# Three places in the order of a two-layer encoder's mixer: the spread of the norm's row, the state products, the second rotary queries

## The chip, the cores and the metric

The kernel runs on one core of a Trainium2 chip. The metric is the time of one execution on the device in microseconds (us); lower is better. A run of the kernel gives one time, and the median of several is compared.

## The reference, cut to what matters

Two layers act on 576 columns of tokens: 512 of a new prompt and 64 of a running stream. A layer is a feed-forward stage, a mixer and a second feed-forward stage, each with a norm in front and behind:

```
x = x + 0.5 * post1(SwiGLU_1(pre1(x)))
h = pre2(x); z = h @ w_in[l]
mix = concat[MLA(512) | HGRN2(256) | chunk-gMLP(256)] @ w_out[l]
x = x + post2(mix)
x = x + 0.5 * post3(SwiGLU_2(pre3(x)))
```

The change lies in the mixer. MLA is attention with four heads, in which queries have a plain and a rotary part, and keys and values come from a compressed latent, for the running stream also from a cache of 256 rows. HGRN2 is a gated recurrence with a matrix state, S_new = exp(b_last) * S + (k * exp(b_last - b))^T v in chunks. A norm needs, for each token, 1/sqrt(mean of squares), which is then multiplied into everything computed from the token.

## The kernel before, in words

**Layout.** x stands as eight tiles of 128 features by 576 tokens; the tokens are two halves of 288 columns (`HALF`). Each fp32 matrix is split into a rounded high part and a rest, so that one product is three matrix multiplications (`three`). PSUM has one pool of eight banks, tag `mm`, from which every product, transpose and column sum takes its bank (`mm`, `sm`); a bank comes free when the engine that copies it out has done so. SBUF is one pool of 57 equal slots.

**How the order is made.** The order is written by hand as a planner in the code. The main line emits the big products; smaller chains are Python generators that are put into a list with a due time (`spawn`). The planner has a clock `self.t`, to which each emitted product adds an estimate: its columns divided by 2400 (in us), at least 0.107. After each group of products `tick` emits every generator step that is due, and a step says with `yield v` that its next one is due v later on that clock. Where the main line needs a result, `until` emits the step with the earliest due time, again and again, while the clock stands still apart from what the steps themselves add:

```
    def until(self, done):
        while not done():
            self.step(min(self.bg, key=lambda q: q[0]))
```

The framework then builds one queue for each engine. Emission order is its priority; where it reckons an instruction not to be ready, a later one may go ahead. At run time each engine takes its queue in that order.

**The norm in front of the mixer.** `post` finishes a half of the stage before and emits its eight parts of h (1.3 of the clock apart for the second half); then `pre_stats` waits 3.97 (first half) or 7.0 (second half), takes column sums of squares with TensorE, scales them on VectorE (`m`, L209), takes the power -0.5 on GpSimd (`rn`, L151), and after `yield 3.11` spreads the row over 128 partitions with three transposes (`spread`, tile `bc`) and copies it to `rbc` with ScalarE (L215). The mixer's first products, four `u` banks for each half, run over eight groups of 12 multiplications (1.44 of the planner's clock each). `zout(z, o, half)` needs `rbc` and empties the four banks; its first line is

```
        self.until(lambda: hf in self.stats_done)
```

For the first half `zout` stands right behind the last group of that half; for the second half it stands behind `natural(nch, 0, 512)`, whose eight groups of three products of 512 columns count 0.64 each. After that `hgrn` starts.

**The state part.** In `hgrn`, behind the levels, `ed[m]` (two tiles) is transposed in five pieces each (tile `tp`), copied by ScalarE to `kdn[m]` (L799) and `kd` (L803), one m after the other with `yield 1.5`. Then ten state products `su` follow 1.2 apart, in the order m = 0, m = 1 for each of five token tiles, each with two VectorE updates, the first and last also with DMAs of the state to HBM, eight in a layer. Behind them come five `out(i)`, 3.2 apart: products `o`, a group norm (ScalarE square, VectorE sum, GpSimd power, VectorE `on`, L847), and 9.0 later transposes into `mixh` and `mixl`. `gates` polls until `ed` is there, and then has ScalarE do five gelu and five silu in a row.

**The values and rotary queries.** `value(j)` is six products of 512 columns into one bank and one VectorE copy (L1171); j = 0 to 4 are new tokens, 5 and 6 the cache. `rope(u)` is a query product of two banks with nine multiplications each (`query`), eight ScalarE copies of 32 rows (`sw`, L1146), two VectorE products with cosT, one GpSimd product with sinT (L1148), a VectorE sum (L1149), and a split with four ScalarE copies and two VectorE differences (`low`, L1156). The order is value 0, 1, rope(4), value 2 to 4, rope(5), value 5, 6. Then for each head `query(h)` (two banks, `q`) with its split (`qh`, `ql`), and keys `k` (three banks).

Of the kernel before, what the change touches and what calls it, by code (L numbers as in the profile page):

```python
# [41 lines left out]
def tcol(i):  # L42
    return 0 if i == 0 else 64 + P * (i - 1)


def twid(i):
    return 64 if i == 0 else P


class Net:  # L50
# [149 lines left out]
    def pre_stats(self, half, wait, sums=None):  # L200
        nc = self.nc
        c0, n = HALF[half]
        nt = 3
        t0 = 3 * half
        rn, rn2, rbc, acc = self.rn, self.rn2, self.rbc, self.acc
        yield wait
        ps = self.colsum(acc, RUNS[half]) if sums is None else sums[:, 2 * half:2 * half + nt]
        m = self.small("m", 6)
        nc.vector.tensor_scalar(m[:, :nt], ps[:, :nt], 1.0 / D, EPS, op0=ALU.mult, op1=ALU.add)  # L209
        r = rn[:, t0:t0 + nt]  # L210
        self.rsqrt(r, m[:, :nt], nt)
        nc.vector.tensor_tensor(rn2[:, t0:t0 + nt], r, r, op=ALU.mult)
        yield 3.11
        bc = self.spread(r, half, None if sums is None else tuple((tcol(i), twid(i)) for i in range(2 * half, 2 * half + nt)))
        nc.scalar.activation(rbc[:, c0:c0 + n], bc, AF.Copy)  # L215
        self.stats_done.add(half)
        if sums is not None and half == 0:

            yield 1.0
            ps = self.sm("ru")  # L220
            self.mul(ps[:, 0:1], rbc[0:1, W2 - P:W2], self.ones[0:1, 0:1], start=True, stop=True)
            nc.vector.tensor_copy(rn[:, 2:3], ps[:, 0:1])
            nc.vector.tensor_tensor(rn2[:, 2:3], rn[:, 2:3], rn[:, 2:3], op=ALU.mult)
# [432 lines left out]
    def hgrn(self, l, zq, zf, vg):  # L656
# [137 lines left out]
        for m in range(2):  # L794
            kdn[m] = self.slot("kdn")[:, :512]
            ps = self.sm("tp")
            for i in range(1, 5):
                self.flip(ps[:, (i - 1) * P:i * P], ed[m][:, tcol(i):tcol(i) + P])
            nc.scalar.activation(kdn[m], ps, AF.Copy)  # L799
            kdn[m, 0] = self.small("kd0", P, 2)  # L800
            ps = self.sm("tp")
            self.flip(ps[:64, :P], ed[m][:, :64])
            nc.scalar.activation(kdn[m, 0][:64], ps[:64, :P], AF.Copy)  # L803
            yield 1.5
        while len(vg) < 5:
            yield 2.07
        for i in (1, 2, 3, 4, 0):
# [244 lines left out]
    def mixer(self, l, gpost, gpre, nxt, packed):  # L1052
# [80 lines left out]
        def query(u):  # L1133
            ps = [self.mm("q"), self.mm("q")]
            for k in range(3):
                for (c0, n), pp in zip(HALF, ps):
                    self.three(pp[:, :n], wqh[k][:, u], wql[k][:, u], qah[k][:, c0:c0 + n], qal[k][:, c0:c0 + n], k == 0, k == 2)
                self.tick()
            return ps

        def rope(u):
            ps = query(u)
            t, sw = self.slot("q"), self.slot("sw")
            for (c0, n), pp in zip(HALF, ps):
                for g in range(4):
                    nc.scalar.activation(sw[g * 32:(g + 1) * 32, c0:c0 + n], pp[(g ^ 1) * 32:((g ^ 1) + 1) * 32, :n], AF.Copy)  # L1146
                nc.vector.tensor_tensor(t[:, c0:c0 + n], pp[:, :n], cosT[:, c0:c0 + n], op=ALU.mult)
            nc.gpsimd.tensor_tensor(sw, sw, sinT, op=ALU.mult)  # L1148
            nc.vector.tensor_tensor(t, t, sw, op=ALU.add)  # L1149

            low = self.slot("low", F32R)
            for e in range(2):
                s, o = slice(64 * e, 64 * e + 64), slice(64 - 64 * e, 128 - 64 * e)
                qr = self.slot("qr", F32R)
                nc.scalar.activation(qr[s], t[s], AF.Copy)
                nc.vector.tensor_tensor(low[s], t[s], qr[s].bitcast(F32), op=ALU.subtract)  # L1156
                nc.scalar.activation(qr[o], low[s].bitcast(F32), AF.Copy)
                a["qr"].append(qr)

        def value(j):  # L1160
            t = self.slot("v")
            ps = self.mm("v")
            for ct in range(2):
                if j < 5:
                    xh, xl = cth[ct][:, tcol(j):tcol(j) + P], ctl[ct][:, tcol(j):tcol(j) + P]
                else:
                    xh, xl = c["ch"][:, ct, (j - 5) * P:(j - 4) * P], c["cl"][:, ct, (j - 5) * P:(j - 4) * P]
                self.mul(ps, xh, uw[0][:, ct], ct == 0, False)
                self.mul(ps, xh, uw[1][:, ct], False, False)
                self.mul(ps, xl, uw[0][:, ct], False, ct == 1)  # L1170
            nc.vector.tensor_copy(t[:, :512], ps)  # L1171
            (a["v"] if j < 5 else a["vc"]).append(t)
            self.tick()
# [4 lines left out]
        rope(4)  # L1178
        for j in range(2, 5):
            value(j)  # L1180
        rope(5)
        self.finish([cg])
        for j in range(5, 7):
            value(j)
        uk = self.chunk([(slice(None), tin["mla_w_uk"][l].rearrange("(k p) h n -> p k (h n)", p=P))], 2, 512)
        at = self.spawn(self.attention(a, c))
        for h in range(HEADS):
# [284 lines left out]
```

## Time and profile before

| | us |
|---|---|
| median of 3 runs | 2253.6 |
| lowest and highest of them | 2252.36, 2254.13 |
| the profiled execution's own time | 2250.07 |
| its span, first to last instruction | 2248.3 |
| TensorE busy in it | 2194.2 |
| mean granted TensorE clock | 0.995 of full speed |

The profiled execution is one run; 1.8 us of its time lie outside its span, and it is 3.5 us below the median. The two mixers reach TensorE at about 415 and 1525 us of the span; times below are counted from the span's start. A row of the timeline gives the start, the duration, the engine, the line, and in brackets how long the engine had been idle and what ended that.

### The profile page before, as it was taken

To read this page: it belongs to the slowest core of one execution; us is meant where nothing else is said; L and a number is where in the kernel's file an instruction comes from. 1 tells how busy PE (TensorE), PEld (TensorE's weight loads), DVE (VectorE), ACT (ScalarE), POOL (GpSimd) and SP (SyncE) were. 2 spreads that over 40 slices of the span, in tenths; PEclk is the share of its full clock that TensorE was granted. 3 is DMA by queue.
4 is the path that set the end of the run, shared out by engine and by line. 5 is a ranking of instruction groups with operands and counts; after the bars stand their busy time and mean duration, and the time that the engine had idled before them with its cause. 6 is when DMAs were issued, how large, how long until landed. Compare 5 with 4: busy or idle time off the path is not lost.

```text
span 2248.3 us, 39455 instructions
## 1 busy us (share of the span) xinstructions
PE 2194.2 (98%) x15988; PEld 2140.4 (95%) x15988; DVE 1540.6 (69%) x2805; ACT 1054.0 (47%) x1877; POOL 69.5 (3%) x96
## 2 busy tenths in 40 slices
PE   8999999999999999999999999999999999999998
PEld 8999999988899999999999999998888999999998
DVE  5888743686766988845498875437867579787543
ACT  7444442344564645443265454325356546444423
POOL 0000000101200000000000000000011000000000
PEclk9999999999999999999999999999999999999999
DMA  7333442222112333344223334423121223323421
GB/s 218 96 97 94 116 143 81 84 69 79 57 57 81 101 98 98 87 130 127 66 81 104 94 93 125 135 76 108 34 85 52 74 98 89 97 86 107 119 71 43
DMA packets 339250, 210.79 MB, mean 94 GB/s; under 512 B 17350, under 2 KB 319420, under 8 KB 339068
## 3 DMA queue, kind: packets, MB, share of 16 engines
q1 hardware_dynamic: 339068, 208.28, 31.0%
q8 instruction: 125, 2.05, 0.4%
q14 instruction: 57, 0.47, 0.1%
HBM read 189.85 MB, written 18.38 MB: 93 GB/s over the span
## 4 chain that ended last, share of the span: by engine, by line
PE 87%; DVE 7%; ACT 3%; POOL 2%; issue 2%; DMA 0%; SPq 0%; POOLq 0%; DVEq 0%; ACTq 0%
PE d L68 25%; PE X L68 20%; PE Q L68 10%; PE u L68 9%; PE R L68 5%; PE n L68 5%; PE wo L68 4%; PE sc L68 1%; PE lv L68 1%; POOL gr L151 1%; PE oT L68 1%; PE q L68 1%; DVE hl L142 1%; DVE wl L127 1%; PE k L68 1%
## 5 line engine op out<-in xcount | busy, mean ns | idle before, releaser
L68 PE MATMUL d<-gh,wh 128*128 128x288 f32 x1408 | 413.5, 297 | 2.7 <-ACT gh L138 2.7
L68 PE MATMUL d<-gl,wh 128*128 128x288 f32 x1408 | 413.9, 295 | 0.0
L68 PE MATMUL d<-gh,wl 128*128 128x288 f32 x1408 | 412.7, 294 | 0.0
L127 DVE TENSOR_TENSOR wl<-wr,wh 128x1024 fp32r<-128x1024 f32 (+3 forms) x190 | 220.3, 1164 | 179.2 <-ACT wh L126 178.8
L126 ACT ACTIVATE wh<-wr 128x1024 fp32r<-128x1024 f32 (+3 forms) x190 | 191.7, 1012 | 315.7 <-PE d L68 167.3
L68 PEld LDWEIGHTS d<-gh,wh 128*128 128x128 f32 x1408 | 262.3, 187 | 3.6 <-ACT gh L138 3.6
L68 PEld LDWEIGHTS d<-gh,wl 128*128 128x128 f32 x1408 | 264.7, 188 | 0.0
L68 PEld LDWEIGHTS d<-gl,wh 128*128 128x128 f32 x1408 | 264.1, 188 | 0.0
L68 PE MATMUL X<-th,wh 128*128 128x288 f32 x864 | 255.7, 296 | 0.0
L68 PE MATMUL X<-tl,wh 128*128 128x288 f32 x864 | 254.9, 295 | 0.0
L68 PE MATMUL X<-th,wl 128*128 128x288 f32 x864 | 254.0, 294 | 0.0
L68 PE MATMUL u<-hl,wh 128*128 128x288 f32 x736 | 219.5, 299 | 4.4 <-DVE hl L142 4.4
L68 PE MATMUL u<-hh,wh 128*128 128x288 f32 x736 | 217.9, 303 | 3.4 <-ACT x L1376 2.4
L68 PE MATMUL u<-hh,wl 128*128 128x288 f32 x736 | 219.2, 299 | 0.6 <-DVE wl L127 0.6
L138 ACT ACTIVATE wh<-wr 128x1024 fp32r<-128x1024 f32 x144 | 151.4, 1055 | 134.7 <-PE R L68 68.4
L139 DVE TENSOR_TENSOR wl<-ws,wh 128x1024 fp32r<-128x1024 f32 x108 | 132.3, 1225 | 95.6 <-ACT wh L138 95.6
L398 DVE TENSOR_TENSOR d<-d,d 128x288 f32<-128x288 f32 x128 | 55.2, 454 | 181.9 <-PE d L68 181.7
L139 DVE TENSOR_TENSOR wl<-wr,wh 128x1024 fp32r<-128x1024 f32 x144 | 174.8, 1220 | 7.2 <-ACT wh L138 6.2
L138 ACT ACTIVATE wh<-ws 128x1024 fp32r<-128x1024 f32 x108 | 114.5, 1060 | 138.3 <-DVE ws L508 100.7
L68 PEld LDWEIGHTS X<-th,wl 128*128 128x128 f32 x864 | 162.7, 188 | 0.0
L68 PEld LDWEIGHTS X<-tl,wh 128*128 128x128 f32 x864 | 162.2, 188 | 0.0
L68 PEld LDWEIGHTS X<-th,wh 128*128 128x128 f32 x864 | 161.9, 187 | 0.0
(363 smaller groups left out, 5401.9 us busy)
## 6 DMA issues: line engine op xcount, KB each, us to landing
wr<-ffn_w_gate SPq DMA_DIRECT2D x144, 256.0 KB, 3.0
wr<-ffn_w_up SPq DMA_DIRECT2D x144, 256.0 KB, 3.4
wr<-ffn_w_down SPq DMA_DIRECT2D x64, 512.0 KB, 4.2
wr<-w_in SPq DMA_DIRECT2D x30, 512.0 KB, 3.7
xd<-x SPq DMA_DIRECT2D x48, 288.0 KB, 2.1
x<-xd SPq DMA_DIRECT2D x48, 288.0 KB, 6.2
wr<-ffn_w_down SPq DMA_DIRECT2D x32, 384.0 KB, 3.5
wr<-ffn_w_gate SPq DMA_DIRECT2D x16, 512.0 KB, 3.8
```

Source lines behind the costliest of these rows:

```text
L68: self.nc.tensor.matmul(out, lhsT, rhs, start=start, stop=stop, skip_group_check=onto)
L126: nc.scalar.activation(hi[:, :a * b], raw[:, :a * b], AF.Copy)
L127: nc.vector.tensor_tensor(lo[:, :a * b], raw[:, :a * b], hi[:, :a * b].bitcast(F32), op=ALU.subtract)
L138: nc.scalar.activation(hi, src, AF.Copy)
L139: nc.vector.tensor_tensor(lo, src, hi.bitcast(F32), op=ALU.subtract)
L142: nc.vector.scalar_tensor_tensor(lo, src, scale, hi.bitcast(F32), op0=ALU.mult, op1=ALU.subtract)
L151: self.nc.gpsimd.tensor_tensor(out, m, self.mhalf[:, :n], op=ALU.pow)
L398: nc.vector.tensor_tensor(d[m][:, sl], d[m][:, sl], ps[hf][:, :n], op=ALU.add)
```

## The change

Three edits, which only alter the order of emission. `self.packed` is false in `pre_stats` only where the stage that follows is the mixer.

```diff
@@ pre_stats
         nc.vector.tensor_tensor(rn2[:, t0:t0 + nt], r, r, op=ALU.mult)
-        yield 3.11
+        yield 3.11 if self.packed else 5.5
         bc = self.spread(r, half, None if sums is None else tuple((tcol(i), twid(i)) for i in range(2 * half, 2 * half + nt)))
@@ hgrn
             nc.scalar.activation(kdn[m, 0][:64], ps[:64, :P], AF.Copy)
-            yield 1.5
+            yield 3.5
         while len(vg) < 5:
@@ mixer
         rope(4)
         for j in range(2, 5):
             value(j)
-        rope(5)
         self.finish([cg])
         for j in range(5, 7):
             value(j)
+        rope(5)
```

## Rows read from the trace of the kernel before

**Rows 1.** The page: busy time of TensorE, and the chain that ended last.

```profile
PE 2194.2 (98%) x15988; PEld 2140.4 (95%) x15988; DVE 1540.6 (69%) x2805; ACT 1054.0 (47%) x1877; POOL 69.5 (3%) x96
PE 87%; DVE 7%; ACT 3%; POOL 2%; issue 2%; DMA 0%; SPq 0%; POOLq 0%; DVEq 0%; ACTq 0%
```

**Rows 2.** Busy time by stretch: length, then busy us (count) of each engine, clock, DMA.

```profile
456.00:596.00 140.00, 132.40 (x826) 116.51 (x825) 105.70 (x308) 65.58 (x137) 15.14 (x19) 1.00 0.24 69
...
740.00:1515.00 775.00, 771.65 (x5790) 770.10 (x5789) 532.00 (x766) 348.12 (x547) 6.59 (x6) 1.00 0.34 101
```

**Rows 3.** TensorE's waits over the span: total us, times, longest.

```profile
PE bc L73 <- POOL rn L151: 8.4, 2, 4.2
PE q L68 <- DVE v L1171: 5.4, 4, 2.7
...
PE su L68 <- ACT kdn L799: 3.9, 2, 2.0
...
PE su L68 <- DVE cn L908: 2.1, 1, 2.1
```

**Rows 4.** Timeline of the first layer, the first half's statistics.

```profile
429.70 0.72 PE L68 MATMUL ss<-ones,acc 128*128 128x1 f32 x6
...
433.68 0.15 DVE L209 TENSOR_SCALAR m<-ss 128x3 f32<-128x3 f32 x1
...
434.81 0.98 PE L73 MATMUL bc<-ident_c,rn 64*128 64x64 f32 x3 [4.15 <-POOL rn L151]
```

**Rows 5.** Three short stretches; the last three columns are granted clock, DMA share, GB/s.

```profile
434.80:438.50 3.70, 3.69 (x16) 3.57 (x17) 3.70 (x11) 2.12 (x5) 0.00 (x0) 0.50 0.43 160
...
546.00:550.00 4.00, 3.88 (x28) 3.88 (x29) 2.18 (x12) 2.32 (x9) 1.52 (x2) 1.00 0.01 4
...
619.50:624.00 4.50, 4.48 (x21) 4.44 (x22) 4.21 (x10) 3.33 (x10) 0.00 (x0) 0.62 0.38 111
```

**Rows 6.** Timeline of the first layer, the second half's spread and what follows it.

```profile
450.46 0.49 PE L73 MATMUL bc<-ident_c,rn 128*128 128x128 f32 x3
...
452.70 1.54 DVE L1050 TENSOR_TENSOR z<-u,rbc 128x288 f32<-128x288 f32 x4
...
457.22 1.28 ACT L672 ACT_TABLE_LOAD   x1
```

**Rows 7.** Timeline of ScalarE in the first layer, around the copies of kdn.

```profile
543.95 1.64 ACT L893 ACTIVATE vg<-vg 128x256 f32<-128x256 f32 x5
545.50 0.57 ACT L799 ACTIVATE kdn<-tp 128x512 f32<-128x512 f32 x1
```

**Rows 8.** Timeline of TensorE in the first layer, the second transposes and their product.

```profile
539.49 0.71 PE L73 MATMUL tp<-ident_c,e 128*128 128x128 f32 x5
...
546.12 0.49 PE L68 MATMUL su<-vg,kdn 128*128 128x128 f32 x2 [1.95 <-ACT kdn L799]
```

**Rows 9.** The chain that ended the stretch 600 to 640: start, us, what.

```profile
614.84 1.45 POOL sw L1148
...
618.79 0.69 DVE v L1171
619.52 2.47 PE q L68 x9
```

**Rows 10.** Timeline of ScalarE and VectorE, where head 0's query is split.

```profile
619.61 0.41 ACT L138 ACTIVATE qh<-q 128x288 fp32r<-128x288 f32 x1
...
621.01 0.82 DVE L139 TENSOR_TENSOR ql<-q,qh 128x288 fp32r<-128x288 f32 x2
```

**Rows 11.** TensorE's waits over the stretch 1530 to 1830, the second layer's mixer.

```profile
PE q L68 <- DVE v L1171: 1.6, 1, 1.6
```

**Rows 12.** Groups by line, 565 to 600 us: us and mean ns, then idle time before.

```profile
L847 DVE SCALAR_TENSOR_TENSOR on<-o,gr,vg 128x64 f32<-128x64 f32 x20 | 4.3, 277 | 3.7 <-POOL gr L151 3.7
...
L141 ACT ACTIVATE mh<-tp,colg 128x128 fp32r<-128x128 f32 (+1 forms) x7 | 2.5, 356 | 2.6 <-PE tp L73 2.3 <-DVE ml L142 0.2
L634 ACT ACTIVATE gsq<-o 128x256 f32<-128x256 f32 x5 | 1.9, 381 | 1.2 <-DVE gs L637 1.2
```

## The prediction, made before the change was run

> **What bounds the kernel now.** First the page: TensorE is busy 98% of the span and makes up 87% of the chain that ended last [rows 1]. VectorE, ScalarE and GpSimd have slack on average, so a reordering can only win back TensorE's idle time. The stretches then say where that lies: between 740 and 1515 us TensorE lacks 3.4 of 775, and a multiplication takes 775/5790 = 0.134 us there; in 456 to 596, inside the first mixer, it lacks 7.6 of 140 [rows 2]. The list of TensorE's waits names the causes. Three groups stand where the three edits act: the spread `bc` behind the power `rn` (8.4 us, two times), the second query behind the copies of the values (5.4), the state products behind `kdn` (3.9) [rows 3]. Together 17.7 us, 0.8% of the span, and no more than that plus the clock is to be had.
>
> The clock adds to it. Behind the 4.15 us wait of `bc` the granted clock is 0.50, that is 1.2 GHz, and 16 multiplications take 3.70 us instead of 16 x 0.134 = 2.1; behind the 2.7 us wait of the second query it is 0.62 on average, and 21 take 4.5 instead of 2.8; behind the 1.95 us wait of a state product it is 1.00 [rows 4, 5, 8]. So the longest waits cost another 1.6 to 1.7 each, the shorter ones nothing.
>
> **Edit 1, the spread: nothing.** It names the largest wait, so it has to be followed by hand. First half: the column sums are emitted one tick before the last group of the half's products, which adds 12 x 0.12 = 1.44 to the planner's clock. Then the main line reaches `zout` for the first half, and its `until` empties the generators with the clock standing still. Before, the spread is due 3.11 - 1.44 = 1.67 past that moment, now 5.5 - 1.44 = 4.06. Its only rival there is the second half's `post`: its remaining parts are due at 1.3, each in turn, and behind them its statistics at 7.0. 1.67 and 4.06 both lie between 1.3 and 7.0. So in both versions the rest of the parts comes first, the spread second, and no product in between: the order of emission up to there is the same, and the 4.15 us of `bc` in the first layer, of which 434.81 - 430.42 = 4.4 us runs from the end of the column sums (VectorE reaches `m` only at 433.68 behind the other half's parts), stays with its slow clock [rows 4, 5]. The second layer has the same code and the same kind of wait (8.4 in two) [rows 3].
>
> Second half: here the spread is emitted by a tick. At 3.11 it falls behind the last group of `u`, at 5.5 two steps of `natural` later (2 x 0.64 = 1.3 on the planner's clock). Nothing waits there now, the row of `bc` has no idle time in front, so there is nothing to gain [rows 6]. What may be lost is hidden: `z` needs the row, ends at 452.70 + 1.54 = 454.24, and ScalarE starts its table for `hgrn` at 457.22 behind the first `natural`; 3.0 us of cover for a shift of 1.3 [rows 6]. Without that cover it would cost 1.3 in each layer. I take 0; bounds 0 and +2.6.
>
> **Edit 2, the state products: -3.9.** The second transposes are done at 540.2, but ScalarE holds its queue with gelu and silu until 545.59 and only then copies `kdn`, to 546.07; the product of m = 1 stands waiting 1.95 us [rows 7, 8]. The edit moves the second transposes 2 later, the first product of m = 0 and m = 1 about 4 later on the planner's clock. The ten matrix multiplications and their 20 VectorE updates move along, and the eight state DMAs; behind these on the SP queue stand loads of weights and of cosT, wanted only by the rotary queries of the stretch behind 600 [rows 9], so their cost is nothing; if that lead were gone, rope(4) would wait by the same 4. The copy of `kdn` may now stand behind a square (0.38) and one norm's worth of small ScalarE work, about 1 us later; the product comes 4 us later, so 4 - 1 = 3 is more than the 1.95. The wait goes, in both layers: -3.9 [rows 3]. What is late next is the bank for a later state product, which VectorE frees with `cn` (2.1 us) [rows 3]. That chain starts from `natural` products that themselves come 1.95 earlier, so I let it stand as it is; bounds: 0 if it takes back all, -3.9 - 2.1 = -6.0 if it goes as well.
>
> **What follows from edit 2: +2.0.** The five `out(i)` and their transposes also come about 4 later, a little over one spacing of 3.2, so one out more falls among values and rotary queries. One out costs VectorE 4 x 0.277 and more, ScalarE 0.381 + 2 x 0.356 = 1.1 [rows 12]. Between 600 and 619.5 the chain runs through ScalarE's `sw` copies, GpSimd, VectorE and back and TensorE hangs on its end [rows 9], so work put into these queues can lengthen it. No row shows how much lands in gaps. I take +1.0 for each layer; bounds 0 and +2.2 (1.1 on each of the two engines, one after the other) each.
>
> **Edit 3, the cached values first: -3.6.** No instruction is added: 12 products and two copies change places with one rope (18 multiplications, 12 ScalarE, 5 VectorE, one GpSimd). VectorE works in the order given, so the copies of values 5 and 6 now stand between the parts of rope(5), which wait for ScalarE and GpSimd: `sw` ends at 616.29, value 5 is copied at 618.79, and the bank it frees lets the second half of `query(1)` start at 619.52, 2.7 late [rows 9]. With values 5 and 6 in front, both copies (0.69 each) fall into the time in which VectorE waits for rope(5), and TensorE passes 619.52 - 2.7 = 616.8 without a stop. It then does nine multiplications of `query(1)` and six of `k`, 15 x 0.134 = 2.0, to 618.8, and there lacks a bank again: all are held by `q` and `k` of head 0, which ScalarE and VectorE split behind rope(5), at 619.61 and 621.01 [rows 10]. With the two copies out of VectorE's way the first `ql` comes 0.7 to 1.4 earlier, and half of 0.82 later the bank is free, at 620.0 to 620.7. The new wait is 1.2 to 1.9; I take 1.5, which is nearer to the 1.95 behind which the clock stayed at full speed than to the 2.7 [rows 5]. Queued behind it are the rest of `k(1)` and head 0's scores. First layer: -2.7 - 1.7 + 1.5 = -2.9; bounds -4.4 and 0. Second layer: the same wait is 1.6 [rows 11]; I take off under half, -0.7, bounds -1.6 and +0.6 (rope(5)'s product is emitted two values later, and ScalarE could start late). Sum -3.6.
>
> A page bears on the 1.7. The Trainium skill, "TensorE: Matmul & The Clock Gate", section "HAM oscillation", says that an idle gap of TensorE shuts its clock to half rate for what follows, but counts only gaps longer than this one. By it the 2.7 us wait would cost itself alone and the sum be 1.7 smaller, -3.8. This trace shows 0.62 behind that wait, so the row decides.
>
> **Sum.** 0 - 3.9 + 2.0 - 3.6 = -5.5 us: 2250.07 becomes 2244.6 for an execution like the profiled one, whose span would be 2242.8. The median of the runs lies 3.5 above it: 2253.6 - 5.5 = **2248.1**. That is 0.24%; about 0.2%, 4.5 us, is what a measurement can tell from no change.
>
> **The rivals.**
> - Edit 1 bites. If the build's own ordering lets a few products of the next half pass the spread, 2.39 of planner's clock is some 20 multiplications, 2.7 us: the wait falls from 4.15 to 1.5 and the clock stays. 2.7 + 1.55 = 4.2 for each layer, 8.5 together: 2239.6. For: it is the largest wait. Against: the emission does not change. 0.10.
> - The gain is handed on. The wait for `kdn` reappears at the bank behind `cn`, or the outs take what rope gains: about -1, 2252.6. For: that wait of 2.1 us stands on the same state products [rows 3]. 0.20.
> - The clock is not won back. If TensorE's new stop at `k(1)` is as long as the old one, half speed follows as now, and 1.7 of edit 3 is lost: 2249.8. For: rows 5 leave open what a wait between 1.95 and 2.7 does. 0.12.
> - Slower. One mechanism: the shifted outs hold their banks among the values and queries until their norm is done, and TensorE meets a new wait of the size of `bc`'s, 4.15 with 1.55 of slow clock, in each layer: +11.4 - 5.5 = +5.9, 2259.5. It decides from 5.0 for each layer. For: VectorE stands idle 3.7 us before the `on` of this stretch, for GpSimd, so a bank is held long [rows 12]. 0.12.
>
> **Numbers.** The forecast has 0.46, and nine tenths of it lie beyond 4.5 us, with rival one: 0.51 faster. Rivals two and three and the rest of the forecast: 0.37 within 0.2%. Slower: 0.12. Likeliest own range 2243 to 2252. The bounds of the terms reach from -6.0 - 4.4 - 1.6 = -12 to +2.6 + 4.4 + 0.6 = +8; the 8-in-10 range takes in rival one and stops short of rival four: 2239.5 to 2256.
>
> **What would show it.** In the new profile: `bc` behind `rn` still about 8.4 in two (edit 1 does nothing); no wait of `su` for `kdn`; no wait of `q` for `v` L1171 at the second query, but one of `k` for `ql` or `qh` of 1 to 2 us, with the clock at 1.00 behind it; waits on `on` not above today's. The forecast is wrong if `bc`'s wait shrinks, or if waits of `v`, `q` or `u` for `on` grow by several us.

## The result, and the profile after

The changed kernel takes 2265.8 us (median of four runs, 2262.3 to 2266.6) against 2253.3; the ratio is 1.0053, with a 95% interval of 1.0035 to 1.0070. It is slower by 12 us, where 5.5 less were forecast. The profiled execution took 2262.28 us with a span of 2260.5, 12.2 longer than before.

The page after, its line of busy time:

```profile
PE 2203.1 (97%) x15988; PEld 2149.3 (95%) x15988; DVE 1540.2 (68%) x2805; ACT 1054.5 (47%) x1877; POOL 71.3 (3%) x96
```

The same 15988 instructions keep TensorE busy 8.9 us longer than in [rows 1]; the other engines' work is the same. So 8.9 of the 12.2 us are not waits, but instructions that run longer, and 3.3 are more idle time. Some ends of multiplications are modelled, so the split is rough; but it says where to look: at the granted clock.

TensorE's waits after, in the form of [rows 3] (total us, times, longest):

```profile
PE bc L73 <- POOL rn L151: 8.4, 2, 4.2
PE u L68 <- DVE ml L139: 4.9, 2, 2.5
PE sc L68 <- ACT kth L138: 4.4, 2, 2.2
...
PE q L68 <- DVE v L1171: 3.9, 2, 2.0
PE q L68 <- DVE on L847: 3.7, 2, 1.9
PE tp L73 <- DVE ctl L139: 2.9, 2, 1.5
```

The spread's wait stands as it was. The state products wait for `kdn` no more, nor for the bank behind `cn`; transposes wait 2.9 for `ctl` in place of 0.9. New are a unit of q_a behind `ml`, head 0's scores behind the split of its keys, and a query behind `on`; the query behind `v` is a single wait of 2 us in each layer now.

What follows such a wait is seen in stretches of 4 us, the first layer (us, busy us and multiplications, granted clock, DMA share, GB/s):

```profile
576.10:580.10 4.00, 3.97 (x20) 0.65 0.17 45
592.00:596.00 4.00, 3.91 (x26) 1.00 0.46 139
597.60:601.60 4.00, 3.96 (x19) 0.57 0.83 266
616.80:620.80 4.00, 3.94 (x19) 0.68 0.42 124
629.00:633.00 4.00, 4.00 (x30) 1.00 0.00 0
```

and the second layer:

```profile
1689.70:1693.70 4.00, 3.96 (x18) 0.57 0.07 12
1710.00:1714.00 4.00, 4.00 (x19) 0.57 0.79 268
1729.10:1733.10 4.00, 3.93 (x20) 0.74 0.42 125
1741.30:1745.30 4.00, 3.97 (x15) 0.58 0.01 4
```

But for the one from 592.0, which has no wait ahead of it, the stretches begin where a wait ends: for `ml` (576.1, 1689.7), `on` (597.6, 1710.0), `v` (616.8, 1729.1) and `kth` (629.0, 1741.3). Seven of eight run partly at 1.2 GHz, behind waits of 1.7 to 2.5 us; the eighth, from 629.0, is at 1.00 although its wait was 2.2 us.

The start of the n-th multiplication, counted from the first of each trace, after minus before (us). Where the order differs it is not the same product in both, so values inside the mixers are good to about half a us:

```
position before:  540    561    569    577    596    606    620    629 to 1533
after - before:   1.75  -0.91  -0.56   4.65   6.34   6.72   5.07   5.94 to 5.89
position before: 1652   1671   1688   1697   1709   1730   1739 to the end
after - before:   5.86   3.74   7.98   6.91   6.34   8.33  12.2
```

1.1 us were there before the first mixer. Edit 2 wins its 2 us in each layer as forecast, to be seen at 561 (2.7) and 1671 (2.1). At 577 and at 1688 they are lost twice over. The last step, 8.33 to 12.2 between 1730 and 1739, is the second layer's wait for `kth` and the half clock behind it.

### The profile page after: what moved, and what is told of

It reads as the page before. It is cut to its first block, busy times and chain, and to the rows that moved or that the text cites. A ratio compares the mean times of both kernels' runs of the same rounds, so it can differ in the third digit from the quotient of the medians.

```text
span 2260.5 us, 39439 instructions
## 1 busy us (share of the span) xinstructions
PE 2203.1 (97%) x15988; PEld 2149.3 (95%) x15988; DVE 1540.2 (68%) x2805; ACT 1054.5 (47%) x1877; POOL 71.3 (3%) x96
## 4 chain that ended last, share of the span: by engine, by line
PE 86%; DVE 7%; ACT 3%; POOL 2%; issue 2%; DMA 0%; SPq 0%; POOLq 0%; DVEq 0%; ACTq 0%
PE d L68 25%; PE X L68 20%; PE Q L68 10%; PE u L68 9%; PE R L68 5%; PE n L68 5%; PE wo L68 4%; PE sc L68 1%; PE lv L68 1%; POOL gr L151 1%; PE oT L68 1%; PE q L68 1%; DVE hl L142 1%; DVE wl L127 1%; PE k L68 1%
```

## What stands at 576 us

TensorE and VectorE of the changed kernel there (start, us; in brackets idle time and what ended it):

```profile
572.83 0.48 PE L68 MATMUL su<-vg,kd 64*128 64x128 f32 x2
573.24 0.44 PE L73 MATMUL tp<-ident_c,kp 128*128 128x128 f32 x2
576.13 0.40 PE L68 MATMUL u<-hh,wh 128*128 128x288 f32 x1 [2.45 <-DVE ml L139]
```

```profile
575.01 0.87 DVE L864 SCALAR_TENSOR_TENSOR uv<-uv,gr,cmlp_v_g 128x64 f32<-128x64 f32 x4 [0.95 <-POOL gr L151]
575.80 0.28 DVE L139 TENSOR_TENSOR ml<-tp,mh 128x128 fp32r<-128x128 f32 x1
576.11 0.29 DVE L821 SCALAR_TENSOR_TENSOR st<-st,eb,su 64x64 f32<-64x64 f32 x1
576.43 0.69 DVE L139 TENSOR_TENSOR ccl<-tp,cch 128x512 fp32r<-128x512 f32 x1
577.04 0.28 DVE L877 SCALAR_TENSOR_TENSOR oc<-cm,colg,uv 128x64 f32<-128x64 f32 x1
```

Counted from the trace, all eight banks are held at 575.0: two by the unit before, one by a gated product's transposes, two by the last state products, two by the transposes of the cached latents (`ck`) and keys (`kp`), one by `cm`. All but the unit's two wait for VectorE next, and it takes them in its queue's order: it stands behind `uv`, which waits for GpSimd's power. The transposes of the caches are due at a fixed time of the planner's clock; the state products, moved by 4, have run into them: the last product starts at 572.83, behind the transposes of `ck` from 571.43. Before, they were just through: the last product started at 566.90, its updates ended at 572.48, and the transposes of `ck` began at 572.50.

## Experiments: each edit alone

**Edit 1 alone.**

```diff
-        yield 3.11
+        yield 3.11 if self.packed else 5.5
```

> Only the first edit (the yield in front of the spread). Theory S (the state products' move made the kernel slower): no change, 0 +- 3 us, with the two waits of bc for rn still 4.2 us each, since the first half's spread is emitted at the same place. Theory V (the order of values and rope did): the same. Rival (the spread's later place delays what starts the recurrence): +3 us or more, with waits of dq and lv above the 0.4 to 0.8 of before.

Measured: 2251.3, ratio 0.9992 (0.9982 to 1.0001), no change. `bc` waits as before:

```profile
PE bc L73 <- POOL rn L151: 8.3, 2, 4.2
```

**Edit 2 alone.**

```diff
             nc.scalar.activation(kdn[m, 0][:64], ps[:64, :P], AF.Copy)
-            yield 1.5
+            yield 3.5
```

> Only the second edit (3.5 instead of 1.5 behind each transpose of ed). Theory S: +6 to +12 us: the two waits of su for kdn (1.95 each) go, and in their place come waits of u and q of 1.7 to 2.5 us behind VectorE, each with some 4 us of clock at half speed. Theory V: -2 to -4 us, the waits for kdn gone and nothing in their place.

Measured: 2266.7 (2259.6 to 2267.5), ratio 1.0048 (1.0032 to 1.0064), within the error the whole loss. The five executions are two at 2259.6 and 2260.2, at a mean granted clock of 0.991, and three at 2266.7 to 2267.5, at 0.986 to 0.987; the median stands in the upper group, so the ratio says more. The waits of one from the lower group:

```profile
PE q L68 <- DVE on L847: 5.1, 4, 2.0
PE u L68 <- DVE ml L139: 4.9, 2, 2.5
```

**Edit 3 alone.**

```diff
-        rope(5)
         self.finish([cg])
         for j in range(5, 7):
             value(j)
+        rope(5)
```

> Only the third edit (values 5 and 6 in front of rope(5)). Theory S: -1 to -4 us, the waits of q for v L1171 (2.7 and 1.6) replaced by a shorter one. Theory V: +6 to +12 us, with a new wait of sc for kth of 2.2 us in each layer and half clock behind it.

Measured: 2251.5, ratio 0.9994 (0.9985 to 1.0003), no change. The query's wait for `v` is gone from the list; in its place stands

```profile
PE sc L68 <- ACT kth L138: 5.1, 2, 3.3
```

with 3.3 us in the first layer and a stretch at 0.68 behind it:

```profile
624.00:628.00 4.00, 3.99 (x18) 0.68 0.00 0
```

ScalarE does rope(5)'s copies first and splits head 0's keys only at 623.3. The wait moved on, and its clock with it.

**Edits 2 and 3.**

> The second and third edit without the first. Both theories: as the full change, +9 to +14 us, since the first edit does nothing; if it comes out under +5, the first edit has a share.

Measured: 2265.0, ratio 1.0050 (1.0035 to 1.0065): edit 2 alone, within the error. Edit 2 is the cause; what is open is what in it.

## Experiments: banks or outs, and how much is the clock

**Edit 2, the caches' transposes 4 later as well.**

```diff
 def caches(self, l, c):
...
-        yield 14.0
+        yield 18.0
```

> Edit 2 alone, and with it the transposes of the cached latents and keys come 4 later on the planner's clock as well (18 in place of 14), so that they stand where they stood to the last state products in the kernel before. Theory B (banks): edit 2 loses because the last state products meet those transposes, and the banks of both wait for VectorE; here the wait of a unit for ml, 2.45 us in each layer, shrinks to under 1.2, the half-clock stretches behind it at 577 and 1690 go, and the time falls from 2266.7 (edit 2 alone) by 5 to 9 us to 2258 to 2262. Rival O (outs): the loss comes from the five outs that are pushed among the values and queries, whatever the caches do; then the time stays at 2264 to 2268 and a query still waits about 2 us for on.

Measured: 2257.1, ratio 1.0021 (1.0011 to 1.0030). By the ratios about half of the loss goes, with the outs due where edit 2 puts them; the unit's wait for `ml` is gone from the list, and where it was the clock is 1.00. The queries' waits for `on` fall too, from 5.1 to 1.4, the longest from 2.0 to 0.7: rival O, which had them stay at 2, fails, and most of that wait too hangs on where the caches' transposes stand. What is left shows in a later stretch: a wait of 1.35 us for the rotary keys' split `kptl`, and half clock behind it.

```profile
576.00:580.00 4.00, 4.00 (x34) 1.00 0.19 45
587.20:591.20 4.00, 3.71 (x16) 0.57 0.41 134
```

**Half of edit 2.**

```diff
-            yield 1.5
+            yield 3.5 if m else 1.5
```

> Edit 2 for its second half alone: the transposes of m = 1 stand where they stood before, the state products follow 2 later (yield 3.5 only behind m = 1), half of edit 2's shift of the products and outs. Theory B: products and outs move by 2, and what counts is whether the last ones reach the caches' transposes; the stretch behind them is between the two kernels, 2255 to 2262, with a unit's wait for ml of 0.5 to 1.5 us. Rival T (transposes): the moved transposes do the harm, since the copies of kdn then stand behind ScalarE's other work; here they are not moved and the time is the one before, 2252 to 2255. A third way: a threshold, either 2253 or 2266.

Measured: 2256.2, ratio 1.0014 (1.0004 to 1.0023), in between, as theory B had it, but by other waits than it named: 0.3 us for `ml`, 1.3 for `kpt` in the first layer and 2.4 for `kptl` in the second, among the transposes of the caches and of the rotary keys.

**Work in the wait.** Edit 2 with idle transposes ahead of the unit that waits:

```diff
             self.flip(ps[:, t * P:(t + 1) * P], kp[:, t * P:(t + 1) * P])
+        for _ in range(14):
+            self.nc.tensor.transpose(ps[:, 256:384], kp[:, :P], self.ident)
```

> Edit 2 alone, with 14 more transposes in each layer, into an unused part of the bank of the cached keys' transposes, right ahead of the unit that waits 2.45 us. They add 28 transposes, some 4 us of TensorE's work, and change no result. Theory C (clock): about 4 us of edit 2's loss is not the two waits but the half clock behind them; with TensorE at work instead of waiting the clock stays at 1.00 behind 577 and 1690 and the time falls by some 4 us below edit 2 alone, to 2261 to 2264, although work is added. Rival W (waits alone): the clock doesn't follow the wait; the time is that of edit 2 alone or up to 4 longer, 2266 to 2271.

Measured: 2257.9, ratio 1.0023 (1.0014 to 1.0033): 8.8 us less than the median of edit 2 alone, 5.6 by the ratios, on another chip, with 28 transposes more.

**The same work where nothing waits.**

```diff
                     ps = self.mm("wo")
+                    if k0 == 4 and mm == 3 and hf == 0:
+                        for _ in range(14):
+                            nc.tensor.transpose(ps[:, 320:448], self.ident, self.ident)
```

> Edit 2 alone with the same 14 transposes in each layer, but where TensorE has no wait: ahead of a product of w_out, behind the mixer. The control to the run with them in the wait. Theory C (clock): these transposes only cost their time, 28 x 0.15 = 4.2 us, and the half clock behind the waits stays: 2268 to 2272. Rival P: any 28 transposes, wherever they are, change the time as much, because the build orders other things differently with them; then about 2258, as with the ones in the wait.

Measured: 2262.0, ratio 1.0044 (1.0029 to 1.0059), which neither theory gave. So the three, edit 2 alone, the work in the wait and the work elsewhere, were run once more on one chip.

> Edit 2 alone once more, on one chip with the next two, since it was timed on another chip than the kernels with added transposes and its five runs there fell into two groups (2259.6 to 2260.2 at a granted clock of 0.991, 2266.7 to 2267.5 at 0.986 to 0.987). Theory C (clock): the groups are those executions in which the clock fell behind more or fewer waits; the median lies between 2258 and 2267, and within the runs the lower clock goes with the longer time. Rival W: the edit costs the same at any clock, 2263 to 2267 here too.

> Edit 2 alone with the 14 transposes in the wait of each layer (28 x 0.109 = 3.1 us of work, by the trace). Theory C: 3 to 7 us below edit 2 alone on this chip, and 5 to 8 below the same work elsewhere. Rival W: the work fits into the wait, nothing else changes: the time of edit 2 alone within 1 us, and 3 below the same work elsewhere.

> Edit 2 alone with the same 28 transposes behind the mixer, where TensorE doesn't wait. Both theories: 3 us above edit 2 alone on this chip. If it comes out below edit 2 alone again, as it did across two chips, then adding work anywhere moves the clock in other stages too, and the two comparisons above are no measure of the one wait.

Measured: edit 2 alone 2263.4 (2262.0 to 2266.0; ratio 1.0048, 1.0035 to 1.0061), work in the wait 2257.4 (2252.9 to 2258.1; 1.0020, 1.0011 to 1.0029), work elsewhere 2262.4 (2258.6 to 2264.6; 1.0040, 1.0027 to 1.0053). The work in the wait takes 6.0 us off, within theory C's 3 to 7. The same work elsewhere comes out 5.0 above it, where theory C had 5 to 8. The first layer's two stretches, edit 2 alone:

```profile
575.20:579.20 4.00, 3.95 (x18) 0.58 0.18 45
595.40:599.40 4.00, 3.90 (x19) 0.61 0.80 278
```

and with the work in the wait:

```profile
578.20:582.20 4.00, 3.90 (x29) 1.00 0.18 45
597.00:601.00 4.00, 3.91 (x32) 1.00 0.80 278
```

29 multiplications in place of 18 in the same 4 us, and 32 in place of 19. The first wait is down to 0.93 us, with transposes in the time that was idle:

```profile
575.68 1.69 PE L586 MATMUL tp<-ident_c,kp 128*128 128x128 f32 x14
578.30 0.40 PE L68 MATMUL u<-hh,wh 128*128 128x288 f32 x1 [0.93 <-DVE ml L139]
```

The second wait, a query's for `on`, is as long as ever (1.96 us at 597.1), and the clock stays at full speed behind it all the same. The earlier pair of traces, edit 2 alone and the work in the wait on two other chips, agrees with this pair on all four places (both layers).

The work elsewhere came out 1 us below edit 2 alone, where 3 above was expected (the two intervals overlap). By what was written ahead of it, added work then moves the clock in other places too, and the 6.0 us is no clean measure of these waits. Where it stands the work costs 1.5 us in each layer, 14 x 0.109; but the profiled execution of edit 2 alone has a half-clock stretch at 1142 us, outside the mixers, which costs it 3.1, and that of the work elsewhere has none. The last section comes back to that stretch. The profiled execution with the work in the wait has it too, so it makes no difference between those two.

What the traces do show is where the clock fell. Between 540 and 660 us and between 1650 and 1770, TensorE was at 1.2 GHz for 6.8 us in all in the kernel before, for 27.3 in the changed kernel (where waits for `v` and `kth` come on top), for 17.1 in both traces of edit 2 alone, for 13.6 in both with the work elsewhere, and not at all in both with the work in the wait. Half of 17.1 - 6.8 is 5.1 us, my estimate of what half clock adds to edit 2; it is near the 6.0.

## Experiments: the wait that edit 1 aimed at

**Units ahead of the row.** The kernel before, with products put where edit 1 wanted them:

```diff
-        for hf in (0, 1):
-            o = self.units(chs, hf)
-            if hf == 0:
-                self.zout(z, o, 0)
+        o = self.units(chs, 0)
+        o1 = self.units(chs[:2], 1)
+        self.zout(z, o, 0)
+        o = o1 + self.units(chs[2:], 1)
+        o1 = None
```

> The kernel before with the mixer's first units in another order: behind the first half's four units come the second half's products of the first two units, then the first half is scaled by its row, then the other two units. So products really stand between the column sums and the spread, which edit 1 aimed at and did not do. If the reading of edit 1 is right (the row's wait is there only because nothing may be emitted between), the two waits of bc behind rn, 8.3 us together, and the half clock behind each go, in part to small waits of a unit for VectorE's parts: the time falls by 4 to 9 us to 2244 to 2249. Rival: TensorE follows VectorE's parts of the second half there anyway, with four or with two units, and the waits only spread: within 2 us of the time before.

Measured: 2247.4 (2242.3 to 2251.6), ratio 0.9977 (0.9967 to 0.9987), 5 us faster than before, and so faster than both kernels. The column sums end at 432.3 and products of the second half fill the time to 436.3. The row, and the stretch around it:

```profile
436.69 0.63 PE L73 MATMUL bc<-ident_c,rn 64*128 64x64 f32 x3 [0.44 <-POOL rn L151]
```

```profile
436.00:440.00 4.00, 3.33 (x23) 1.00 0.40 152
```

0.44 us in place of 4.15, at full clock where [rows 5] had 0.50. Over the row's stretch the trace gains 4.2 us in the first layer and 4.35 in the second.

**The same with work in two more waits**, in each layer 12 transposes ahead of the first state product of m = 1 and 12 ahead of query(1):

```diff
+                if i == 1 and m == 1:
+                    for _ in range(12):
+                        nc.tensor.transpose(ps[:, 256:384], self.ident, self.ident)
...
             ps = [self.mm("q"), self.mm("q")]
+            if u == 1:
+                for _ in range(12):
+                    nc.tensor.transpose(ps[0][:, 320:448], self.ident, self.ident)
```

> The version with the units ahead of the first half's row (2247.35), with 12 more transposes ahead of the first state product of m = 1, where TensorE waits 1.95 us for kdn, and 12 ahead of query(1), where it waits 2.67 and 1.62 us for a bank of the values. Theory C (clock): the work lies in waits and the half clock behind them goes, 3 to 4 stretches of some 2 us: 2239 to 2244. Rival W (waits alone): nothing is won, and what of the 7 us of transposes doesn't fit into the waits is paid: 2247 to 2250.

Measured: 2244.4 (2242.1 to 2248.3), ratio 0.9969 (0.9958 to 0.9979). By the ratios that is 0.0008 below the version without it, with intervals that overlap: not shown to be better, and theory C's 2239 to 2244 is just missed.

**That work alone, in the kernel before.**

> The kernel before with the same 48 transposes alone. Theory C: the half clock behind query(1) in the first layer goes (1.7 us), that behind the state products is seen in some executions only; the time is 1 to 4 us below the one before, 2248 to 2252. Rival W: the time before or up to 2 us more, 2252.5 to 2255.

Measured: 2254.0, ratio 1.0010 (1.0000 to 1.0020); nothing won, as rival W had it. The work ahead of the state product pushed `su` into another wait, of 1.8 us, and the clock fell behind that one:

```profile
559.90:563.90 4.00, 3.91 (x20) 0.62 0.66 202
```

Behind `query(1)` the clock did stay up in this trace, as theory C expected, but the time shows no gain from it. Here the work put in one wait made the next.

## Why the prediction was wrong

- **Edit 1, nothing:** right. `until` in `zout` sets the order; alone it gave 0.9992. And the wait was to be had: with products really in between, the kernel is 5 us faster.
- **Edit 2, -3.9:** right as far as it reached. The waits for `kdn` went, and the trace gains 2.7 us by 561 and 2.1 by 1671. One term was off: the copy of `kdn` for m = 1 came 5.5 us later (545.50 to 551.04), not 1; that the wait went all the same is because its product came 7.1 later (546.12 to 553.18), not 4.
- **What is late next:** this step failed. I asked it of the one bank that already showed a wait, the one behind `cn`, and let it stand at nothing; that wait in fact went. The bank that came late belongs to no state product: it is that of a q_a unit, at 576, where the moved products meet the caches' transposes: 2.45 us of wait in each layer, 4.9 in the place of 0. Which banks are held when the last moved product lands was not counted.
- **What follows from edit 2, +2.0:** mis-sized. A query waits for `on` 1.7 us in the first layer and 1.95 in the second, where I had put 1.0 in each for work in the queues. With the unit's wait it is 4.9 + 3.7 us of new waits for both layers, against 2.0. And it is not the outs' work alone: with the caches later and the outs due as late, the wait of 1.7 in the first layer is gone.
- **The clock, "the shorter ones nothing":** failed. I read it off one wait of 1.95 us behind which the clock stayed at 1.00 [rows 5]. Behind the four waits of 1.7 to 2.5 us that edit 2 makes it fell to half in both traces of edit 2 alone. Work in the first wait of each layer took 6.0 of 11.8 us back on one chip, and the traces' half clock comes to 5.1. So about half of edit 2's loss is half clock, as an estimate. The Trainium skill, "TensorE: Matmul & The Clock Gate", section "HAM oscillation", describes waits that come again and again, each with a fall of the clock behind it. The trace agrees, but with waits shorter than those that the section counts (1.73 us, then 0.57).
- **Edit 3, -3.6:** its own wait went, but the new one stands at head 0's scores, 3.3 us in the first layer and 1.8 in the second, not 1.5 at the keys' second half. Alone, the edit changes nothing that can be told from 0 (0.9994), so the new wait costs what was won. I had followed the banks of `q`, not ScalarE's order, in which the split of the keys now comes behind rope(5)'s four copies.
- **The rival that came true** is the slower one, in kind: banks held among values and queries, with slow clock behind. Its price was 11.4 for both layers at one place each; here it is two places in each, and 576 was not among those that it named. Its 2259.5 is the nearest of the forecast and the rivals to the 2265.8 measured, but it was made of other waits.

Open: why one wait of about 2 us is followed by half clock and another isn't; and how the 5.8 us that stay with the work in the wait divide among the waits left.

## What to carry to other kernels

When a group of instructions is moved later, list what holds a bank at the time when its last member lands, and which engine reads those banks in what order; the cost appears there and not where the old wait was. Count a wait of about 2 us in a dense TensorE stream at up to twice its length, since the half clock that may follow costs more: in the stretches above 18 to 20 multiplications stand in 4 us in place of about 30, some 1.5 us. And before tuning a due time, see whether the planner can act on it at all: here a blocking call set the order, and products had to be emitted ahead of that call.

## What was not expected of the hardware

The granted clock fell behind waits of 1.7 to 2.5 us, but not by their length: a state product's wait of 1.95 us was followed by 1.00 in [rows 5], and the wait at the same place, just as long, by 0.57 in the version with the units ahead:

```profile
543.50:547.50 4.00, 3.90 (x17) 0.57 0.01 4
```

These are one execution of each. That the kernel decides it isn't shown, for one place outside the mixers says otherwise. All 16 traces have the same wait there, 2.01 us for `hl` at about 1140; behind it the clock fell in ten of them and stayed in six, the kernels before and after among the six. Edit 2 alone, in its first run and in its second:

```profile
1144.59 0.40 PE L68 MATMUL u<-hl,wh 128*128 128x288 f32 x1 [2.01 <-DVE hl L142]
1144.60:1148.60 4.00, 4.00 (x31) 1.00 0.52 192
```

```profile
1141.93 0.41 PE L68 MATMUL u<-hl,wh 128*128 128x288 f32 x1 [2.01 <-DVE hl L142]
1142.00:1146.00 4.00, 4.00 (x19) 0.55 0.52 192
```

The same kernel and the same wait, and 31 multiplications or 19 in the 4 us behind it. So one trace with the clock at 1.00 behind a wait, as the prediction had at 546 us, doesn't show that such a wait costs nothing.

In both traces with work in the first wait, the clock stayed up behind the second one too, 19 us later, that was as long as before.
